# Retention norm by GpSimd and VectorE, and the second gathered chunk's x1, places and pace

## The chip, the cores and the metric

The kernel runs on one core of a Trainium2 chip. The metric is the time of one execution in microseconds on the device, as the median of the runs shown. A core has engines that run side by side, each through its own list of instructions in order: TensorE (PE in the profile; its weight loads are PEld), VectorE (DVE), ScalarE (ACT), GpSimd (POOL) and SyncE (SP), which only issues transfers. Sixteen DMA engines move the data; GpSimd issues the gathers, SyncE the rows of weights, ScalarE a few others.

## The reference, cut to what matters

One layer of a decoder for 512 prompt tokens and 32 sample tokens, D = 1024. First a mixer: four retention heads of width 128 beside a convolution of width 31, then an output projection and a layer norm, which gives x1. Then PEER, an expert retrieval: each token takes, for each of 8 heads, 16 of 16384 single-neuron experts and adds their outputs. The two places that the change touches:

```python
def head_norm(x):
    mu = jnp.mean(xf, axis=-1, keepdims=True)
    var = jnp.mean(jnp.square(xf - mu), axis=-1, keepdims=True)
    return ((xf - mu) * lax.rsqrt(var + LN_EPS)).astype(x.dtype)
...
u = jnp.take(peer_u, idx, axis=0)
act = jax.nn.gelu(jnp.einsum('phkd,pd->phk', u, xb), approximate=False)
vv = jnp.take(peer_v, idx, axis=0)
return jnp.einsum('phk,phkd->pd', gate * act, vv)
```

## The kernel before

**Tokens.** They are worked in groups: chunk 0 (128 prompt tokens), the 32 samples, chunk 1 (128), and the last 256 prompt tokens. The mixer runs for chunk 0 first, then for the other 416 tokens together. A retention chunk is `retain` (L731): `scores` (L355), `attend` (L363), `advance` (L372) and `head_norm` (L320), whose result `gate_heads` (L339) transposes on TensorE (L342) and multiplies with the gate (L343). The kernel leaves the decay of the queries out of `attend`, so its heads come out scaled by a factor per row and head; `head_norm` puts it right with the constants gq and gq2. Beside this, `silu_gate` (L243) makes the gate from a sigmoid on ScalarE (L252) and a step on VectorE (L254).

**PEER in two ways.** The first three groups fetch their experts: `gather` (L583) goes through slots k; for each, GpSimd issues an indirect transfer (L591) of 128 rows of 8 KB (u and v of one expert per token), VectorE multiplies u with x1 and sums (L597, the dot), ScalarE makes the gelu and the weight (L605, L606), VectorE adds weight times v to the accumulator (L611). Chunk 0 has 128 slots, the samples 32 (four heads' groups lie side by side in the 128 partitions), chunk 1 128. The last 256 tokens meet all experts on TensorE: `scores_of` (L815) reads a row `ut` of 512 KB and multiplies it (L822), `build` (L895) makes the selection matrices from one-hot steps on ScalarE (L902, L904) and VectorE (L906, L910) and small products (L915), and `v_products` (L936) reads a row of 512 KB and adds its products (L939) into four banks of PSUM.

**The last part.** `run` (L623, called at L1041) interleaves two generators: `phases` (L982), which issues the value rows e = 0 to 127, the second `build` and the last 32 score rows, and `fetched` (L1020), which finishes chunk 0, then gathers the samples, then chunk 1. `finish` (L614) adds x1, makes the layer norm (`layer_norm`, L446) and stores.

**Places.** A gathered slot lies in a tile of 128 x 2048 from a pool: `gp` has three; chunk 0 has one more in `gx` for its first 48 slots, chunk 1 one more in `gx2` (for k % 4 == 3). The pool `dn`, one buffer for each name, holds x1g (the x1 of the group at work, read back from `x1_dram`), and yt (the result ahead of its store).

**The pace.** `units` collects one TensorE instruction for each value row from e = 48 on (L980), each score row of the last 32 (L824) and each second of the last rows (L1017): 112 in all. For chunk 1, slot k waits for unit (k - 28)*15//14, where that is not negative (L588 to L595).

**The order.** Each engine's list is written by a scheduler that plans the whole program ahead, not by the order of the Python lines; `behind` and `hold` tie single instructions to others (the dots of chunk 0 from slot 48 on stand behind steps of the norms, `steps["p"]`). So an edit in one place can move instructions elsewhere.

## Time and profile before

| | us |
|---|---|
| median of 3 runs | 1550.36 (1547.07 to 1553.19) |
| the profiled execution | 1559.73 |
| its span, first to last instruction | 1558.0 |
| PE busy | 1479.0 (95%) |
| DVE busy | 1226.4 (79%) |
| ACT busy | 579.5 (37%) |
| POOL busy | 390.4 (25%) |
| DMA | 505.85 MB, mean 325 GB/s |

A row of the timeline gives start, duration, engine, line, operation, tiles, and in brackets how long the engine stood idle before it and what released it. A row of the chain of work that ended last gives start, duration and what it was. A busy TensorE need not be at its peak, since ends of matmuls are modelled.

### The profile page before, as it was taken

To read this page: it belongs to the slowest core of one execution; us is meant where nothing else is said; L and a number is where in the kernel's file an instruction comes from. 1 tells how busy PE (TensorE), PEld (TensorE's weight loads), DVE (VectorE), ACT (ScalarE), POOL (GpSimd) and SP (SyncE) were. 2 spreads that over 40 slices of the span, in tenths; PEclk is the share of its full clock that TensorE was granted. 3 is DMA by queue.
4 is the path that set the end of the run, shared out by engine and by line. 5 is a ranking of instruction groups with operands and counts; after the bars stand their busy time and mean duration, and the time that the engine had idled before them with its cause. 6 is when DMAs were issued, how large, how long until landed. Compare 5 with 4: busy or idle time off the path is not lost.

```text
span 1558.0 us, 20737 instructions
## 1 busy us (share of the span) xinstructions
PE 1479.0 (95%) x7046; PEld 1006.9 (65%) x7046; DVE 1226.4 (79%) x3151; ACT 579.5 (37%) x1633; POOL 390.4 (25%) x329
## 2 busy tenths in 40 slices
PE   6999989987999999899999999999999999999996
PEld 6978657555766668788878885444566666644332
DVE  3869989978756999999977989567776766766666
ACT  2224443225111333333534799424993111111111
POOL 2001225232321222312231100222223332333430
PEclk9999999998999999999999999999999999999999
DMA  9648786985689779999999723999989999999995
GB/s 351 253 152 353 253 268 235 378 346 173 238 338 346 263 264 355 346 339 350 372 358 355 278 82 130 409 336 424 356 323 403 412 424 414 411 425 411 424 419 218
DMA packets 100120, 505.85 MB, mean 325 GB/s; under 512 B 10248, under 2 KB 21256, under 8 KB 57126
## 3 DMA queue, kind: packets, MB, share of 16 engines
q0 software_dynamic: 42240, 305.12, 50.7%
q1 hardware_dynamic: 51325, 192.05, 32.4%
q10 hardware_dynamic: 6448, 7.36, 1.6%
q8 instruction: 55, 0.90, 0.2%
q14 instruction: 52, 0.42, 0.1%
HBM read 499.12 MB, written 5.80 MB: 324 GB/s over the span
## 4 chain that ended last, share of the span: by engine, by line
PE 40%; DVE 24%; DMA 18%; issue 10%; ACT 4%; POOL 3%; SPq 0%; POOLq 0%; DVEq 0%; ACTq 0%
PE sp L822 13%; PE pB L939 13%; DMA g<-in_uv_dram,Ib 7%; DVE acc L611 6%; PE mm L487 5%; DMA g<-in_uv_dram,I 5%; DVE g L597 4%; PE mm L200 4%; POOL g L591 3%; PE mm L915 2%; DMA uv<-in_ut_dram 2%; DMA g<-in_w_in_dram 2%; ACT off L902 1%; DMA uv<-in_uv_dram 1%; DVE B L910 1%
## 5 line engine op out<-in xcount | busy, mean ns | idle before, releaser
L822 PE MATMUL sp<-x1T,uv 128*128 128x256 f32 x2048 | 464.7, 383 | 5.7 <-DMA uv<-in_ut_dram 4.2
L611 DVE SCALAR_TENSOR_TENSOR acc<-g,wgt,acc 128x1024 f32<-128x1024 f32 x285 | 364.6, 1279 | 92.6 <-ACT wgt L606 91.2
L822 PEld LDWEIGHTS sp<-x1T,uv 128*128 128x128 f32 x2048 | 386.8, 192 | 76.3 <-issue 22.1
L591 POOL DMA_INDIRECT g<-in_uv_dram,I x128 | 170.7, 1333 | 461.6 <-DVE acc L611 257.9
L605 ACT ACTIVATE act<-act 128x1 f32<-128x1 f32 x288 | 57.6, 200 | 585.2 <-DVE g L597 584.9
L591 POOL DMA_INDIRECT g<-in_uv_dram,Ib x128 | 158.7, 1240 | 443.7 <-DVE acc L611 127.7
L597 DVE SCALAR_TENSOR_TENSOR g<-g,x1g 128x1024 f32<-128x1024 f32 x160 | 195.3, 1223 | 79.3 <-DMA g<-in_uv_dram,Ib 55.5
L200 PE MATMUL mm<-x1T,w 128*128 128x384 f32 (+1 forms) x512 | 178.3, 504 | 1.5 <-ACT score L536 1.3
L597 DVE SCALAR_TENSOR_TENSOR g<-g,x 128x1024 f32<-128x1024 f32 x128 | 154.8, 1215 | 28.5 <-DMA g<-in_uv_dram,I 28.4
L939 PE MATMUL pB<-uv,Ga 128*128 128x512 f32 x352 | 159.9, 599 | 1.8 <-DMA uv<-in_uv_dram 1.7
L902 ACT ACTIVATE off<-row,e1T 128x128 bf16<-128x128 bf16 x512 | 157.6, 388 | 1.0
L200 PEld LDWEIGHTS mm<-x1T,w 128*128 128x128 f32 x512 | 97.2, 192 | 73.4 <-issue 40.0
L939 PE MATMUL pB<-uv,Gd 128*128 128x512 f32 x256 | 115.2, 598 | 2.3 <-DMA uv<-in_uv_dram 1.6
L939 PEld LDWEIGHTS pB<-uv,Ga 128*128 128x128 f32 x352 | 65.0, 190 | 80.5 <-issue 64.1
L939 PE MATMUL pB<-uv,Gb 128*128 128x512 f32 x256 | 113.5, 597 | 2.4 <-DMA uv<-in_uv_dram 1.9
L939 PEld LDWEIGHTS pB<-uv,Gd 128*128 128x128 f32 x256 | 46.7, 190 | 70.6 <-issue 62.7
L939 PEld LDWEIGHTS pB<-uv,Gb 128*128 128x128 f32 x256 | 47.3, 190 | 58.0 <-issue 53.0
L915 PEld LDWEIGHTS <-A 128*128 128x128 bf16 x1536 | 60.7, 96 | 31.8 <-issue 17.6
L915 PE MATMUL mm<-B,A 128*128 128x96 bf16 (+1 forms) x1536 | 64.3, 191 | 9.3 <-DVE Gc L956 5.4
L910 DVE TENSOR_TENSOR B<-M,gtT 128x768 bf16<-128x768 bf16 (+1 forms) x192 | 69.2, 418 | 4.5 <-PE mm L915 4.5
L939 PE MATMUL pB<-uv,Gc 128*128 128x512 f32 x160 | 72.7, 600 | 0.0
L904 ACT ACTIVATE A<-off 128x1024 bf16<-128x1024 bf16 x64 | 67.4, 1054 | 10.0 <-PE mm L915 9.0
(274 smaller groups left out, 1674.7 us busy)
## 6 DMA issues: line engine op xcount, KB each, us to landing
uv<-in_uv_dram SPq DMA_DIRECT2D x132, 512.0 KB
uv<-in_ut_dram SPq DMA_DIRECT2D x128, 512.0 KB
w<-in_w_in_dram SPq DMA_DIRECT2D x18, 1024.0 KB
w<-in_w_query_dram SPq DMA_DIRECT2D x16, 1024.0 KB
w<-in_w_out_dram SPq DMA_DIRECT2D x7, 1024.0 KB
g<-in_uv_dram,I POOLq DMA_INDIRECT x128
keys<-in_state_retention_dram ACTq DMA_DIRECT2D x4, 512.0 KB
out_dram<-keys SPq DMA_DIRECT2D x4, 512.0 KB
```

Source lines behind the costliest of these rows:

```text
L200: T.matmul(p[:, :n], w[m // 2][:, k, (m % 2) * 128:(m % 2 + 1) * 128], xT[:, k, c0:c0 + n], start=(k == 0), stop=(k == 7))
L487: last = T.matmul(banks_[q][:n, s * 256:(s + 1) * 256], src[:, k, c0:c0 + n], wo[q * 2 + s][:, k0 + k, :], start=(xT is None and k0 == 4 a ...
L591: fetch = G.indirect_dma_start(out=t, out_offset=None, in_=a["uv"], in_offset=bass.IndirectOffsetOnAxis(ap=idx[:, k:k + 1], axis=0))
L597: dot = V.scalar_tensor_tensor(t[:, :D], t[:, :D], 1.0, x1, op0=OP.mult, op1=OP.mult, accum_out=act[:, 0:1])
L605: S.activation(act[:, 1:2], act[:, 0:1], AF.Gelu)
L611: V.scalar_tensor_tensor(acc, v, wgt, acc, op0=OP.mult, op1=OP.add)
L822: mm = T.matmul(sp[:, i], u[:, k], x1T[:, k, NG2:], start=(k == 0), stop=(k == 7), skip_group_check=True)
L902: S.activation(off[:, t], row, AF.Abs, bias=e1T[:, t1 + t:t1 + t + 1])
L904: S.activation(A, off, AF.Relu, bias=1.0, scale=-1.0)
L910: V.tensor_tensor(B[:, q], M, pairs_of(gtT[:, q], t1).to_broadcast([128, TB // 2, ne, 2]), op=OP.mult)
L915: mm = T.matmul(pt[:, t % nt], A[:, t - t1], B[:, q, (t - t1) // 2, :, t % 2], start=(q == 0), stop=(q == 2))
L939: ps_.append(T.matmul(pB[b][q], W[:, b * 128:(b + 1) * 128], vt[:, q * 512:(q + 1) * 512], start=False, stop=(e == NK - 1), skip_group_che ...
```

## The change

**The norm.** The factor per row and head cancels in a norm except at the small constant, so the constant is divided by its square (`ce`, made on the host) in place of multiplying the variance by gq2 and the root by gq. The root is then an addition and a power on GpSimd. Each head's result is one step on VectorE, (x - mean) * root, in place of a bias (nb) and one step on ScalarE. `steps[kind]` is now the last of these steps.

**The gathers.** Chunk 1's x1 is read into the place of chunk 0's x1 (the name `x1_0`), issued from slot 24 of the samples on, behind the end of the first build, in place of a `dn` tile after the samples are done. The pool `dn` now holds one tile of the size of a slot: first the samples' x1 in one half and the results of chunk 0 and of the samples in the other, then the fifth place of chunk 1's slots (k % 5 == 4; `gx2` is the place of k % 5 == 3). Chunk 1's result lies in a `gp` tile and is stored by ScalarE's queue. The pace is (32, 11, 10): slot k waits for unit (k - 32)*11//10, and 32 slots have none.

```diff
-PACE = (28, 15, 14)
+PACE = (32, 11, 10)
...
-    parts["gq_p"] = np.exp((i + 1.0)[:, None] * lg)
-    parts["gq2_p"] = np.exp(2 * (i + 1.0)[:, None] * lg)
+    parts["ce_p"] = EPS * np.exp(-2 * (i + 1.0)[:, None] * lg)
...
         rs = small("hrs", [128, H])
-        V.tensor_mul(rs[:n], mv[:n, :, 1], cc("gq2_" + kind)[:n])
-        rsqrt(rs[:n], rs[:n])
-        V.tensor_mul(rs[:n], rs[:n], cc("gq_" + kind)[:n])
-        nb = small("hnb", [128, H])
-        steps[kind] = V.scalar_tensor_tensor(nb[:n], mv[:n, :, 0], -1.0, rs[:n], op0=OP.mult, op1=OP.mult)
+        G.tensor_add(rs[:n], mv[:n, :, 1], cc("ce_" + kind)[:n])
+        G.tensor_tensor(rs[:n], rs[:n], mhalf[:n].to_broadcast([n, H]), op=OP.pow)
         on = small("on", [128, 512])
         for h in range(H):
-            S.activation(on[:n, h * DH:(h + 1) * DH], po[:n, h * DH:(h + 1) * DH], AF.Identity,
-                         bias=nb[:n, h:h + 1], scale=rs[:n, h:h + 1])
+            steps[kind] = V.tensor_scalar(on[:n, h * DH:(h + 1) * DH], po[:n, h * DH:(h + 1) * DH], mv[:n, h, 0:1],
+                                          rs[:n, h:h + 1], op0=OP.subtract, op1=OP.mult)
...
-            spare = gx if x1 is x1_0 and k < KX else (gx2[0] if gx2 and len(slots) == 128 else None)
-            t = (spare if spare is not None and k % 4 == 3 else gp).tile([128, 2 * D], F32, name="g")
+            if x1 is x1_0:
+                pool = gx if k < KX and k % 4 == 3 else gp
+            else:
+                pool = (gp, gp, gp, gx2[0], dn)[k % 5] if len(slots) == 128 else gp
+            t = pool.tile([128, 2 * D], F32, name="g")
...
     def fetched():
-        t = dn.tile([128, D], F32, name="yt")
+        both = dn.tile([128, 2 * D], F32, name="g")
+        x1s, t = both[:, :D], both[:, D:]
         finish(x1_0, [acc0[:, 0:512], acc0[:, 512:]], 128, [(0, 128, o[0][0, 0:128])], t)
...
+        for k, _ in enumerate(gather(x1s, Ig["s"], GTg["s"].rearrange("p h k -> p (h k)"), ac, range(NS))):
+            if k == FREE + 4:
+                x1b = per.tile([128, D], F32, name="x1_0")
+                behind(nc.scalar.dma_start(x1b, x1_dram[NS:NS + 128]), fence[0])
             yield
...
+        ac = per.tile([128, D], F32, name="acc")
+        yield from gather(x1b, Ig["b"], GTg["b"].rearrange("p h k -> p (h k)"), ac, range(128))
+        t = gp.tile([128, 2 * D], F32, name="g")[:, :D]
+        finish(x1b, [ac[:, 0:512], ac[:, 512:]], 128, [(0, 128, o[0][0, 128:256])], t, True, nc.scalar)
```

More of the change, by code (lines that the diff above doesn't have):

```diff
@@ L67, in _consts @@
     parts["kc_p"] = (DH ** -0.5) * np.exp((C - 1.0 - i)[:, None] * lg)
-    parts["gq_p"] = np.exp((i + 1.0)[:, None] * lg)
-    parts["gq2_p"] = np.exp(2 * (i + 1.0)[:, None] * lg)
+    parts["ce_p"] = EPS * np.exp(-2 * (i + 1.0)[:, None] * lg)
     for n, v in (("kc_s", (DH ** -0.5) * np.exp((SQ - 1.0 - si)[:, None] * lg)),
-                 ("gq_s", np.exp((si + 1.0)[:, None] * lg)), ("gq2_s", np.exp(2 * (si + 1.0)[:, None] * lg)),
+                 ("ce_s", EPS * np.exp(-2 * (si + 1.0)[:, None] * lg)),
                  ("blk", (sb[:, None] == np.arange(SB)[None, :]) * 1.0)):
@@ L612, in gather, with finish @@
             yield
-    def finish(x1, f, n, dsts, t, table=False):
-        for q in range(2):
-            c = slice(q * 512, (q + 1) * 512)
-            V.scalar_tensor_tensor(t[:n, c], x1[:n, c], ALPHA, f[q][:n], op0=OP.mult, op1=OP.add)
+    def finish(x1, f, n, dsts, t, table=False, q=nc.sync):
+        for h in range(2):
+            c = slice(h * 512, (h + 1) * 512)
+            V.scalar_tensor_tensor(t[:n, c], x1[:n, c], ALPHA, f[h][:n], op0=OP.mult, op1=OP.add)
         layer_norm(t, n, ln2[0], ln2[1], table=table)
         for p0, p1, dst in dsts:
-            nc.sync.dma_start(dst, t[p0:p1])
+            q.dma_start(dst, t[p0:p1])
     def run(*gens):
```

22 lines of the change are left out of this document (9 added, 13 removed).

## The prediction

> **What bounds the kernel now.** I read the span by stages first, then GpSimd's list of gathers, then the chain of work that ended last, at the two places that the change touches. The columns of the first view are the stretch, its length, the busy time of TensorE, its weight loads, VectorE, ScalarE and GpSimd, the granted clock, the DMA share and GB/s.
> ```profile
> span 1558.0 us, 20737 instructions
> ...
> 350.00:380.00 30.00, 20.16 (x103) 15.93 (x102) 26.29 (x60) 21.99 (x44) 6.57 (x8) 0.77 0.43 147
> ...
> 1100.00:1140.00 40.00, 39.73 (x317) 20.62 (x318) 30.81 (x72) 39.84 (x118) 10.00 (x7) 1.00 0.93 343
> 1140.00:1180.00 40.00, 40.00 (x359) 28.39 (x358) 27.85 (x60) 35.99 (x108) 12.01 (x10) 1.00 0.89 333
> 1180.00:1540.00 360.00, 354.09 (x1013) 187.63 (x1012) 242.14 (x308) 54.70 (x213) 112.92 (x91) 1.00 1.00 412
> 1540.00:1558.00 18.00, 7.70 (x18) 3.04 (x17) 14.75 (x25) 2.06 (x4) 0.00 (x0) 0.86 0.23 87
> ```
> Four things are to be seen. From 1180 to 1540 the DMA engines are full: 412 GB/s at a share of 1.00, so this stretch lasts as long as its bytes. From 1100 to 1180 they are not full (343 and 333 GB/s), while ScalarE, which builds the selection matrices, has no room (39.84 of 40). From 350 to 380 nothing is full: TensorE works 20.16 of 30 us and waits for the rest, which is where the heads are normalised. And in the last 18 us VectorE works 14.75.
>
> The gathers of the second chunk (slots 0 to 127) in GpSimd's list: the last without a pace (slot 27), the first with one (slot 28), and slot 127.
> ```profile
> 1129.19 1.67 POOL L591 DMA_INDIRECT g<-in_uv_dram,Ib  x1 [1.20 <-DVE acc L611]
> 1141.72 0.94 POOL L591 DMA_INDIRECT g<-in_uv_dram,Ib  x1 [10.87 <-PE pB L939]
> ...
> 1528.94 0.94 POOL L591 DMA_INDIRECT g<-in_uv_dram,Ib  x1 [2.79 <-PE pB L939]
> ```
> Slot 28 stood 10.87 us for its unit of TensorE, in the stretch where the DMA engines had room. I call 1141.72, the end of unit 0, T0. There are 112 units: 76 from rows 48 to 123 of the value products (L980), 32 score rows (L824), 4 from the last rows (L1017).
>
> **Part 1, the norm's root.** Before, the chain of a head norm is VectorE (statistics, times gq2), GpSimd (add, power), VectorE (times gq, then nb), ScalarE (four steps). After, it is VectorE (statistics), GpSimd (add, power), VectorE (four steps). The chain of work that ended last, ahead of TensorE's wait for the second norm of the three long chunks:
> ```profile
> 363.88 1.39 ACT on L335 x4
> ...
> 371.11 0.62 DVE blk L254
> 371.72 1.19 DVE acc L611
> 372.91 0.60 DVE blk L343
> 373.51 0.07 DVE hrs L330
> 373.58 1.20 DVE acc L611
> 374.78 0.09 DVE hnb L332
> 374.87 0.03 issue
> 374.89 0.47 ACT on L335
> 375.36 0.05 issue
> 375.40 0.48 PE mm L342
> ```
> The first row is the first norm's four ScalarE steps. They stand in front of the sigmoid that L254 at 371.11 waits for; they go, so L254 comes 1.39 earlier. In the order of instructions after the change, VectorE then has L254, one accumulate, the mask product of L360 and the new steps; L343 and the other accumulate stand behind them. The nearest rows for the mask product, the new step (128x128, read from PSUM), and the small steps that go:
> ```profile
> 369.17 0.68 DVE L360 TENSOR_TENSOR sc<-mm,cst 128x512 f32<-128x512 f32 x1
> ...
> L325 DVE BATCH_NORM_STATS2 hst<-mm x20: 269/282/299, 81.2 to 382.4; 128x6 f32<-128x128 f32 x16, 32x6 f32<-32x128 f32 x4
> ...
> L330 DVE TENSOR_TENSOR hrs<-hrs,cst x5: 145/155/163, 84.4 to 389.2; 128x4 f32<-128x4 f32 x4, 32x4 f32<-32x4 f32 x1
> ```
> I take 0.28 for a new step. From the sigmoid's end to TensorE it was 375.40 - 371.11 = 4.29; it becomes 0.62 + 1.19 + 0.68 + 0.28 + 0.05 = 2.82. With the 1.39 that is 1.39 + 1.47 = 2.9 us. Bounds: nothing, if the sigmoid or the scores come late for another reason, and 9.6, if both of TensorE's waits for a norm go whole:
> ```profile
> 365.32 1.12 PE L342 MATMUL mm<-cst,on 128*128 128x128 f32 x4 [2.95 <-ACT on L335]
> ...
> 375.40 0.48 PE L342 MATMUL mm<-cst,on 128*128 128x128 f32 x1 [6.65 <-ACT on L335]
> ```
> I take 3, near the sum. VectorE gains 20 steps of 0.28 and loses 15 of 0.155: 5.6 - 2.3 = 3.3 us more over five norms. I cost them at nothing: they fall where VectorE has room (26.29 of 30 in the worst stretch), and the first norm's four end before the table load and dots that ScalarE takes next. Without that cover it is 3.3. The norms of chunk 0 and of the samples I cost at nothing as well: TensorE has products of its own in front of their transposes and keeps them in that order. The new GpSimd add reads two operands where the old one read one; GpSimd finishes the root more than 3 us before it is used here, so its price doesn't count.
>
> **Part 2, the second chunk's x1, places and pace.** First the handover from the samples to the second chunk:
> ```profile
> 1026.31 5.50 DMA x1g<-x_dram
> ...
> 1035.18 1.18 POOL L591 DMA_INDIRECT g<-in_uv_dram,Ib  x1 [5.43 <-ACT act L605]
> ...
> 1063.22 0.94 POOL L591 DMA_INDIRECT g<-in_uv_dram,Ib  x1 [2.76 <-DVE acc L611]
> ```
> Today the chunk's first dots wait for its x1 (5.50 us), which waits for the samples' last reads. After, x1 lies ready, and slots 5 to 8 can be gathered some 10 us earlier; but slot 4's place holds the samples' x1 and result, so its gather waits for the samples' output. That output is ready at about 1036 (VectorE mixes four dots into the samples' norm), its transfer is below the 5.50 of a transfer four times its size, so slot 4 is issued at 1038 to 1041, against 1035.18 now. In GpSimd's order slot 4 stands behind slot 8, and slot 9, which needs slot 4's place, right behind it. By 1063 (slot 12 now) I expect the two kernels level. From there five places beat four: now slots 13 to 27 take until 1129 with four places and slot 28 stands 10.87; with five I expect slot 32 ready by T0. So four more gathers lie before T0, in the stretch at 343 GB/s: 40 us x (412 - 343) = 2.8 MB of room, 3.2 MB more at 333, for 4.2 MB. Each adds an act and a weight step on ScalarE in front of the build there:
> ```profile
> L605 ACT ACTIVATE act<-act 128x1 f32<-128x1 f32 x288 | 57.6, 200 | 585.2 <-DVE g L597 584.9
> ...
> uv<-in_uv_dram SPq DMA_DIRECT2D x132, 512.0 KB
> ```
> Two such steps are 0.4 us, times four 1.6. Part of it delays T0; I take 1 (between 0 and 1.6).
>
> Now the full stretch. A row is 512 KB, 0.524 MB; a gather is 128 rows of 8 KB, 1.049 MB. **Before**, from T0 to slot 127's issue (unit (127-28)x15//14 = 106): 106 units and 99 gathers, 55.6 + 103.8 = 159.4 MB in 1528.94 - 1141.72 = 387.2 us, 411.6 GB/s, which agrees with the windows. **After**, slot 32 is at unit 0 and slot 127 at unit (127-32)x11//10 = 104: 104 units and 95 gathers, 54.5 + 99.6 = 154.1 MB, at the same rate 374.4 us. Behind that unit stand 7 units instead of 5. The end of TensorE:
> ```profile
> 1538.88 8.82 PE L939 MATMUL pB<-uv,Gd 128*128 128x512 f32 x20 [1.63 <-DMA uv<-in_uv_dram]
> ...
> 1196.18 3.45 PE sp L822 x16
> 1199.63 3.43 PE pB L939 x8
> ```
> A unit without waits is 3.43. Before: 1538.88 + 8.82 = 1547.70, T0 + 406.0. After: 374.4 + 7 x 3.43 + the 1.63 = T0 + 400.0. That is **6.0** earlier, less 1 for T0: 5.
>
> **The tail.** The last chain on VectorE:
> ```profile
> 1548.00 0.60 DVE lst L453
> 1548.60 1.19 DVE yt L467
> 1549.79 1.32 DVE g L467 x2
> 1551.11 0.62 DVE lst L453
> ```
> Two pieces of other blocks' norms (1.19 + 1.32 = 2.5) stand between the statistics of the last block's halves, since the second chunk's last gather landed late. After, that gather is issued 7 units ahead of the end; with some 12 us to land and be added and 6 to finish it is done about 6 us before TensorE ends, and in VectorE's order the last block's statistics stand alone at the end. Gain 2.5 (0 to 2.5). The output by ScalarE's queue is off the path.
>
> **The sum.** 3 + 5 + 2.5 = 10.5 us. The profiled execution took 1559.73 (1.73 outside its span), 9.4 above the median of the runs, 1550.36; I take the difference from the median: **1539.9**. TensorE's order between 447 and 1180 moves too: two score rows (3.45 us each) go behind the start of the first build, and one row's products more stand behind the last. I cost this at nothing, between -5 and +5.
>
> **Rivals.** (a) *Full anyway.* If the four extra gathers push T0 back by their own bytes, 4.2 MB at 411.6 GB/s = 10.2 us, part 2's 6.0 turns into a loss of 4.2 and only the norm and the tail are left: 3 + 2.5 - 4.2 = 1.3 to, with half pushed back, 6.4 us, so 1544 to 1549. For it: 1040 to 1100 has little room as well. Against: slot 28's wait of 10.87 at DMA engines with room. Chance 0.22.
>
> (b) *TensorE becomes the bound.* With five requests out the engines could run fuller. From T0, 112 units x 3.43 = 384, and some 6 for ScalarE's build up to 1180: TensorE ends at T0 + 390, 16 before now, and with 3 and 2.5 the time is 1529. For it: the full stretch is 412 on average, with windows above it. Against: places don't widen engines that are full. Chance 0.10. The Trainium skill (DMA: Bandwidth & Descriptors, section "Where 436 GB/s comes from") puts the ports' ceiling at 435 GB/s and says that the HBM side binds at about 358; the trace stands above the second (412) and below the first, and at 435 the 154.1 MB would take 354 us (an estimate), less than 104 units of TensorE.
>
> (c) *Slower: the handover starves the chain.* Slot 4's gather waits for an output, slot 9 waits for slot 4 at the head of GpSimd's queue, and VectorE's order has slot 9's dot ahead of slot 7's and 8's accumulates, so for two landings of about 10 us nothing else is released. If the chain is behind the pace at T0, each slot short is a gather more in the full stretch, 1.049 / 0.4116 = 2.55 us. It decides from slot 28 at T0: four slots short are 10.2, the whole gain of 10.5. At slot 24, 8 x 2.55 = 20.4 against 10.5, the time is 1560. For it: two landings in a row without overlap. Against: slot 28 had 11 us to spare. Chance 0.12.
>
> (d) *The norm's gain is lost* and the order's moves cost up to 5: 1543 to 1548. Chance 0.09.
>
> **Numbers.** Forecast, 1533 to 1542.6: 0.45. Below 1533, by (b) or the larger norm bound: 0.12. Half a per cent, 7.8 us, is about what a measurement can tell from no change: faster, below 1542.6, is 0.57; same, to 1558.1, from (a), (d) and the mildest of (c), 0.34; slower, the rest of (c), 0.09. The range 1528 to 1554 leaves 0.1 on either side.
>
> **What would show it.** Norm: no wait of TensorE for the norm's output between 350 and 380, and the mixing products (L487) some 3 us earlier. Handover: slots 5 to 8 issued before slot 4, slot 4 at about 1038. Places: slot 32 standing for TensorE at T0. Pace: slot 127 issued some 375 us after T0, seven units before TensorE's end. Tail: no other norm between the last block's statistics. Wrong would be a released-by-VectorE slot 32 long after T0, or T0 itself late by 10.

## The result, and the profile after

| | before | changed |
|---|---|---|
| median of 6 runs, us | 1550.33 (1543.0 to 1553.19) | 1562.56 (1559.85 to 1575.23) |
| ratio to before, 95% interval | 1 | 1.0095 [1.0068, 1.0123] |
| the profiled execution, us | 1559.73 | 1564.66 |

The change makes the kernel **slower**, by 0.95% with an interval clear of 1: the medians differ by 12.2 us. The forecast was 10.5 faster, and the result lies 8.6 us above the upper end of its range.

The two profiled executions differ by only 4.9 us. That of before was 9.4 over its median, that of after 2.1 over its own: 4.9 + 9.4 - 2.1 = 12.2. So sums over the two profiles come out at 4.9, and what lies early in the span has to be compared over more profiles than two.

The same stretches of the changed kernel (columns as in the prediction):
```profile
span 1562.9 us, 20735 instructions
...
350.00:380.00 30.00, 21.35 (x107) 16.17 (x106) 28.03 (x57) 18.61 (x36) 7.02 (x7) 0.83 0.44 145
1100.00:1140.00 40.00, 37.81 (x332) 19.95 (x332) 32.01 (x68) 39.81 (x119) 13.66 (x10) 0.96 0.98 372
1140.00:1180.00 40.00, 38.56 (x323) 24.46 (x319) 30.88 (x72) 39.78 (x117) 9.79 (x8) 1.00 0.84 313
1180.00:1540.00 360.00, 358.84 (x1138) 196.31 (x1137) 240.64 (x314) 63.00 (x236) 102.83 (x91) 1.00 1.01 414
1540.00:1563.00 23.00, 15.92 (x38) 6.72 (x36) 17.33 (x28) 2.67 (x6) 0.00 (x0) 0.94 0.36 136
```
From 1100 to 1140 the DMA engines move more than before (372 for 343 GB/s), as forecast, but from 1140 to 1180 less (313 for 333), and behind 1180 they are as full as before (414 for 412). TensorE works only 37.81 and 38.56 of the two times 40 us from 1100 (before 39.73 and 40.00), and the end is later.

The gathers in GpSimd's timeline: slots 5, 4, 9, 31, 32 and 127:
```profile
1031.97 1.05 POOL L591 DMA_INDIRECT g<-in_uv_dram,Ib  x1 [8.61 <-ACT acc L609]
...
1045.93 0.94 POOL L591 DMA_INDIRECT g<-in_uv_dram,Ib  x1 [2.58 <-issue]
1063.06 1.68 POOL L591 DMA_INDIRECT g<-in_uv_dram,Ib  x1 [16.19 <-DVE acc L611]
...
1145.35 0.95 POOL L591 DMA_INDIRECT g<-in_uv_dram,Ib  x1 [3.42 <-DVE B L910]
1157.59 0.94 POOL L591 DMA_INDIRECT g<-in_uv_dram,Ib  x1 [11.29 <-PE pB L939]
...
1531.63 0.94 POOL L591 DMA_INDIRECT g<-in_uv_dram,Ib  x1 [1.95 <-PE pB L939]
```
T0, the first gather with a pace, is 1157.59 against 1141.72 before and 1139.7 in the forecast's terms. Slot 32 was ready and stood 11.29 us for its unit of TensorE: five places did bring 32 slots ahead of T0, but T0 itself is **15.9 us late**; 10 was the prediction's sign of being wrong. Behind it the forecast holds: slot 127 at T0 + 374.0 (forecast 374.4), TensorE's end at 1538.51 + 17.42 = 1555.93, T0 + 398.3 (forecast 400.0; before 406.0).

The last chain:
```profile
1538.51 17.42 PE pB L939 x40
...
1555.96 0.71 DVE lst L450
...
1556.69 0.22 DVE lmv L451
...
1556.93 1.41 DVE g L459 x2
...
1558.45 0.75 DVE g L464
1559.20 0.66 DVEq L1095
```
No other block's norm stands between the last block's statistics. TensorE's end to the end of the span is 1562.9 - 1555.93 = 7.0 for 10.3 before (1558.0 - 1547.7). So by the profiles: 15.9 for T0, less 406.0 - 398.3 = 7.7 and 3.3, is 4.9.

For the experiments I cut the way to T0 at two marks: M, the end of the mixing products (L487), and S, the issue of chunk 1's first gather (slot 3's, for the place in `gx2`), which the end of the first build releases. From M to S, before and after (two views, one of each kernel):
```profile
445.28:965.52 520.24, 499.33 (x2783) 399.97 (x2782) 465.89 (x1584) 240.19 (x643) 107.42 (x90) 0.99 0.81 302
```
```profile
440.97:970.14 529.17, 502.78 (x2784) 403.08 (x2782) 467.28 (x1584) 240.28 (x643) 103.58 (x90) 0.98 0.81 299
```
The same work takes 520.2 before and 529.2 after: 8.9 us, in a stretch to which the prediction gave nothing. TensorE is idle for 26.4 us of it in place of 20.9, and busy 3.5 us longer for the same products, at a mean granted clock of 0.98 for 0.99. From S to T0 it is 1141.72 - 965.52 = 176.2 before and 1157.59 - 970.14 = 187.5 after: 11.3 us. M itself is 4.3 earlier. These three make the 15.9.

### The profile page after: what moved, and what is told of

It reads as the page before. It is cut to its first block, busy times and chain, and to the rows that moved or that the text cites. A ratio compares the mean times of both kernels' runs of the same rounds, so it can differ in the third digit from the quotient of the medians.

```text
span 1562.9 us, 20735 instructions
## 1 busy us (share of the span) xinstructions
PE 1485.1 (95%) x7046; PEld 1016.3 (65%) x7046; DVE 1230.2 (79%) x3156; ACT 572.8 (37%) x1613; POOL 383.7 (25%) x329
## 4 chain that ended last, share of the span: by engine, by line
PE 47%; DVE 22%; DMA 14%; ACT 7%; issue 6%; POOL 2%; SPq 0%; DVEq 0%; POOLq 0%; ACTq 0%
PE pB L939 18%; PE sp L822 14%; DMA g<-in_uv_dram,I 7%; DVE acc L611 5%; PE mm L484 5%; PE mm L199 5%; DVE g L597 5%; ACT off L902 3%; DMA g<-in_uv_dram,Is 2%; DMA g<-in_uv_dram,Ib 2%; ACT A L904 2%; PE mm L915 2%; DMA g<-in_w_in_dram 2%; POOL g L591 1%; PE mm L310 1%
## 5 line engine op out<-in xcount | busy, mean ns | idle before, releaser
L822 PE MATMUL sp<-x1T,uv 128*128 128x256 f32 x2048 | 462.7, 383 | 3.9 <-ACT off L902 2.7
L822 PEld LDWEIGHTS sp<-x1T,uv 128*128 128x128 f32 x2048 | 388.4, 192 | 74.7 <-issue 12.4
L597 DVE SCALAR_TENSOR_TENSOR g<-g,x 128x1024 f32<-128x1024 f32 x256 | 311.9, 1221 | 86.8 <-DMA g<-in_uv_dram,Ib 62.7
L591 POOL DMA_INDIRECT g<-in_uv_dram,I x128 | 161.0, 1258 | 472.5 <-DVE acc L611 214.3
L591 POOL DMA_INDIRECT g<-in_uv_dram,Ib x128 | 151.5, 1183 | 458.5 <-PE pB L939 169.2
L939 PE MATMUL pB<-uv,Ga 128*128 128x512 f32 x352 | 158.4, 597 | 0.0
L939 PE MATMUL pB<-uv,Gb 128*128 128x512 f32 x256 | 113.5, 597 | 2.2 <-DMA uv<-in_uv_dram 1.8
L939 PEld LDWEIGHTS pB<-uv,Ga 128*128 128x128 f32 x352 | 65.4, 190 | 75.9 <-issue 66.5
L939 PE MATMUL pB<-uv,Gd 128*128 128x512 f32 x256 | 113.1, 596 | 0.4
L939 PEld LDWEIGHTS pB<-uv,Gd 128*128 128x128 f32 x256 | 47.2, 190 | 66.3 <-issue 58.5
L939 PEld LDWEIGHTS pB<-uv,Gb 128*128 128x128 f32 x256 | 47.2, 190 | 58.4 <-issue 52.5
L939 PE MATMUL pB<-uv,Gc 128*128 128x512 f32 x160 | 76.4, 623 | 0.0
L910 DVE TENSOR_TENSOR B<-M,gtT 128x768 bf16<-128x768 bf16 (+1 forms) x192 | 69.8, 423 | 8.1 <-PE mm L915 8.0
L904 ACT ACTIVATE A<-off 128x1024 bf16<-128x1024 bf16 x64 | 67.4, 1053 | 13.4 <-PE mm L915 12.6
L199 PE MATMUL mm<-g,w 128*128 128x160 f32 (+1 forms) x512 | 69.4, 293 | 1.3 <-DMA w<-in_w_in_dram 1.1
```

Source lines behind the costliest of these rows:

```text
L199: T.matmul(p[:, :n], w[m // 2][:, k, (m % 2) * 128:(m % 2 + 1) * 128], xT[:, k, c0:c0 + n], start=(k == 0), stop=(k == 7))
L591: fetch = G.indirect_dma_start(out=t, out_offset=None, in_=a["uv"], in_offset=bass.IndirectOffsetOnAxis(ap=idx[:, k:k + 1], axis=0))
L597: dot = V.scalar_tensor_tensor(t[:, :D], t[:, :D], 1.0, x1, op0=OP.mult, op1=OP.mult, accum_out=act[:, 0:1])
L822: mm = T.matmul(sp[:, i], u[:, k], x1T[:, k, NG2:], start=(k == 0), stop=(k == 7), skip_group_check=True)
L904: S.activation(A, off, AF.Relu, bias=1.0, scale=-1.0)
L910: V.tensor_tensor(B[:, q], M, pairs_of(gtT[:, q], t1).to_broadcast([128, TB // 2, ne, 2]), op=OP.mult)
```

## The experiments

All times are medians with a ratio to the kernel before that ran on the same chip, and its 95% interval; the other columns come from each kernel's profile. Row 52 is the first value row whose products (L939) use the second build's first tile, `Ga`; it stands a fixed number of products behind unit 0, and unlike T0 doesn't depend on slot 32.

| | ratio | us | M to S | S to row 52 |
|---|---|---|---|---|
| before, profiled twice (e5) | | 1550.33 | 520.2, 520.9 | 205.1, 206.3 |
| changed | 1.0095 [1.0068, 1.0123] | 1562.56 | 529.2 | 216.7 |
| e1 norm alone | 1.0033 [1.0012, 1.0054] | 1555.11 | 528.7 | 202.8 |
| e2 all but the norm | 1.0020 [1.0002, 1.0038] | 1553.46 | 517.4 | 217.7 |
| e3 fifth place from slot 8 | 1.0078 [1.0048, 1.0107] | 1564.02 | 529.5 | 220.6 |
| e4 one key product held | 1.0160 [1.0129, 1.0190] | 1572.68 | 535.9 | 219.4 |
| e6 norm, lists as before | 0.9974 [0.9951, 0.9997] | 1546.63 | 519.1 | 207.2 |
| e7 e3, ScalarE's acts held | 1.0104 [1.0074, 1.0134] | 1569.01 | 525.1 | 211.0 |
| e8 e7 without the norm | 1.0028 [1.0005, 1.0051] | 1553.0 | 521.4 | 210.5 |
| e9 idle copies alone | 1.0047 [1.0021, 1.0073] | 1560.17 | 528.0 | 203.7 |
| e10 x1 in place alone | 0.9984 [0.9962, 1.0006] | 1549.25 | 522.0 | 205.1 |
| e11 e2 with the old pace | 1.0063 [1.0038, 1.0089] | 1562.43 | 518.3 | 219.8 |
| e12 new pace alone | 0.9963 [0.9940, 0.9986] | 1547.0 | 523.0 | 205.3 |
| e13 e14 with e6's norm | 0.9928 [0.9904, 0.9952] | 1539.4 | 518.3 | 204.0 |
| e14 change with four places | 1.0011 [0.9984, 1.0038] | 1554.44 | 532.5 | 209.8 |
| e15 change with e6's norm | 1.0006 [0.9983, 1.0029] | 1550.3 | 517.8 | 219.6 |
| e16 e12 with e6's norm | 0.9947 [0.9921, 0.9973] | 1542.59 | 520.3 | 204.7 |
| e17 e13, fifth place from slot 32 | **0.9910 [0.9889, 0.9932]** | 1537.93 | 522.1 | 203.8 |
| e18 e13, fifth place for slots 0 to 29 | 0.9999 [0.9979, 1.0019] | 1549.9 | 522.2 | 217.7 |

The first theory had two parts. In the head, from M to S, the norm's new step makes the planner order the lists that follow in another way, and that costs; its narrow form was that one product on the sub-keys, which now comes early and stands for its keys, is the cost. At the handover, slot 4's place comes free late and the chain of gathers starves. The rivals: the steps of the norm cost by themselves; the handover's loss is the bytes of four more gathers (rival (a) of the prediction); or the pace or the new x1 is at fault.

**e1, the norm alone; e2, all but the norm.** e1 has before's `gather`, `finish`, `fetched` and pace with the changed `head_norm`; e2 is the reverse.

> The kernel before with the norm's part alone (GpSimd's root, one VectorE step per head); x1, places and pace as before. Theory H (the head loses on TensorE's order): the mixing products end about 4 us earlier, but TensorE's list then has the first products on the sub-keys 13 score instructions sooner, TensorE stands some 6 to 7 us for the keys ahead of 482, and the first build ends, with slot 3's gather of the second chunk, at 969 to 971 instead of 965.5; the time is 4 to 5 us above before's, ratio 1.003. Rival P (the prediction's part 1): 3 us below before's, ratio 0.998. Rival V (the 3.3 us of extra VectorE work count in full, no order effect): 3 us above, with the first key products no later than before.

> The change without the norm's part: before's norm, with x1 in place, five slot places and the pace from slot 32. Theory D (slot 4's dot stands first in VectorE's list, ahead of those of slots 5 to 8): slot 3's gather at 965.5 as before, slot 4 issued at about 1041, VectorE idle for 15 to 17 us around 1040 to 1055, T0 (issue of slot 32) 10 to 12 us after before's 1141.7, slot 127 374 us after T0, TensorE's end 398 us after T0; so the profile's span is within 2 us of before's 1558.0 and the time is 0 to 7 us above before's median, ratio 1.000 to 1.005. Rival F (five places pay, the prediction's part 2): 7 us below before's, ratio 0.995. Rival S (all of the loss is part 2): 12 us above, 1.008.

Each half loses by itself, e1 0.33%, e2 0.20%, and M to S is long only where the new norm is (528.7; 517.4 without). All five norms end before M, so what is lost between M and S is not the time of the norm's own steps.

**e3, the fifth place first used by slot 8.**
```diff
-                pool = (gp, gp, gp, gx2[0], dn)[k % 5] if len(slots) == 128 else gp
+                pool = ((gp, gp, gp, gx2[0])[k] if k < 4 else (gp, gp, gp, gx2[0], dn)[(k - 4) % 5]) if len(slots) == 128 else gp
```


> The change with one edit: the fifth place (that of the samples' x1 and result) is first used by slot 8 instead of slot 4. Theory D: dots 4 to 7 no longer stand behind a place that waits for the samples' output; VectorE's idle stretch of 16.8 us falls below 8, slot 9 is issued 8 to 11 us earlier than 1063, T0 comes 8 to 11 us earlier (1147 to 1150), all behind T0 as in the changed kernel, time 8 to 11 us below the changed kernel's, 1552 to 1555. Rival B (T0 is held by the second build on ScalarE and by TensorE's order, not by the gathers): T0 within 3 us of 1157.6 and the time within 3 us of 1562.6.

Slots 9 and 32 in GpSimd's timeline:
```profile
1050.49 0.94 POOL L591 DMA_INDIRECT g<-in_uv_dram,Ib  x1 [1.35 <-DVE acc L611]
...
1163.67 0.93 POOL L591 DMA_INDIRECT g<-in_uv_dram,Ib  x1 [23.83 <-PE pB L939]
```
VectorE's longest wait for a landing at the handover, first changed, then e3:
```profile
1058.06 1.23 DVE L597 SCALAR_TENSOR_TENSOR g<-g,x 128x1024 f32<-128x1024 f32 x1 [16.79 <-DMA g<-in_uv_dram,Ib]
```
```profile
1069.94 1.23 DVE L597 SCALAR_TENSOR_TENSOR g<-g,x 128x1024 f32<-128x1024 f32 x1 [8.05 <-DMA g<-in_uv_dram,Ib]
```
In the changed kernel slot 4's dot stands in VectorE's list ahead of those of slots 5 to 8, and VectorE stands 16.79 us for its landing. In e3 slot 9 comes 78.6 us after S in place of 92.9, but the trouble is halved and moved, not cured: VectorE stands 8.05 us for a later landing. T0 is no earlier: slot 32 now stands 23.83 us for TensorE. So at T0 it is not the gathers that are late but TensorE's own list; whether the handover makes that list late is taken up behind e18.

**e4, the early product on the sub-keys held back.** TensorE's waits ahead of that product, first changed, then e6, then before (timeline of each):
```profile
480.44 2.90 PE L530 MATMUL mm<-keys,qs 128*128 128x128 f32 x12 [6.69 <-DMA keys<-in_keysT_dram]
```
```profile
475.03 1.95 PE L541 MATMUL mm<-keys,qs 128*128 128x128 f32 x16
```
```profile
482.95 2.02 PE L533 MATMUL mm<-keys,qs 128*128 128x128 f32 x16 [0.58 <-DMA keys<-in_keysT_dram]
```
In the changed kernel's list 8 score instructions (L822) stand ahead of it, before 21; so it meets its keys in flight and stands 6.69 us.
```diff
+    behind(kmm[first_key], smm[23])
```


> The change with one edit: the first product on the sub-keys of the long chunks is held behind the 24th score instruction in TensorE's list (before: 21, changed: 8), nothing else. Theory H: TensorE's wait of 6.7 us ahead of 480 goes, the end of the first build (slot 3's gather) moves from 970.1 to 962 to 966, and the time is 4 to 8 us below the changed kernel's. Rival V (the VectorE steps or the gathers' landings, not TensorE's order, set the end of the first build): slot 3's gather stays within 1.5 us of 970.1 and the time within 2 us of the changed kernel's.

It got worse: 1.0160, M to S 535.9. The narrow form fell: that wait is not the cost, or what the hold moves costs more.

**e5, before again.** The unchanged kernel, profiled a second time, in one execution of 1554.14 us.

> The kernel before, unchanged, for a second profile of it. Theory J (the profiled execution of before was an untypical one): the mixing products end near 435, as in the run with the places alone, whose instructions up to there are the same, and not at 445.3; the span is 1545 to 1551 instead of 1558.0; from the end of the mixing to slot 3's gather 517 to 521, from there to T0 (slot 28) 174 to 177, from T0 to TensorE's end 402 to 407. Rival: the span is 1556 to 1560 again, and the 10 us belong to the kernel.

M at 442.41 for 445.28, M to S 520.9 for 520.2, S to T0 177.4 for 176.2: in these two profiles the stretches repeat within 1.2 us, the head up to M does not. In e2, whose lists are those of before up to M, M is at 435.01. So M in a single profile says little about the norm.

**e6, the norm with the lists as before.** GpSimd's root in all five norms; the step on VectorE in four, while the first of the three long chunks keeps nb and ScalarE's four steps. With that the lists of TensorE, VectorE, ScalarE and GpSimd from M to S are those of before, instruction by instruction.
```diff
+        if (1, 1, 0, 1, 1)[len(calls) - 1]:
+            on = small("on", [128, 512])
+            for h in range(H):
+                steps[kind] = V.tensor_scalar(on[:n, h * DH:(h + 1) * DH], po[:n, h * DH:(h + 1) * DH], mv[:n, h, 0:1],
+                                              rs[:n, h:h + 1], op0=OP.subtract, op1=OP.mult)
+            return on
```


> The norm's part in four of the five norms (GpSimd's root in all five; ScalarE's four steps with the factor and the offset stay in the first long chunk's norm alone), x1, places and pace as before. TensorE's list behind the norms is then that of before (21 score instructions ahead of the first product on the sub-keys, 488 ahead of the first build; with all five norms changed 8 and 472). Theory O (the norm's part costs by the order of the lists behind it, not by its own work): from the end of the mixing to slot 3's gather 517 to 522 as before, against 528.7 in the run with the whole norm part; time within 2 us of before's, ratio 0.998 to 1.001. Rival V (the 16 VectorE steps themselves delay what follows): 4/5 of the loss of the whole part, 525 to 528 there, ratio 1.0025 or more.

```profile
436.83:955.97 519.14, 498.39 (x2784) 399.96 (x2782) 466.58 (x1584) 240.50 (x643) 104.93 (x90) 0.99 0.81 303
```
M to S is 519.1, the kernel 0.26% faster than before (4.0 us; the prediction had 3). With all five norms, e1, it is 0.33% slower: 0.59% between two kernels that differ in one norm's four steps.

**e7 and e8, ScalarE's acts held back.** In the changed kernel and in e3 ScalarE's list has more acts ahead of the second build's steps than before's. Here the acts of slots 12 to 33 are held behind the build's steps as in before's list; e7 on e3, e8 on e3 without the norm.
```diff
+    for k, n in ((12, 38), (13, 39), (14, 40), (15, 41), (16, 43),
...
+        behind(acts[k], asteps[n])
```


> The run with the fifth place from slot 8, and one more edit: on ScalarE the activations of the second chunk's slots 12 to 33 are held behind those steps of the second build that stand ahead of the same slots before (slot 12's behind step 7 of the build, slot 13's behind step 8, and so on). Theory A (T0 is late because ScalarE, which has no room in the second build, gets to it some 10 us later, its steps standing behind activations of gathers that have not landed): ScalarE is full from 108 to 112 us after slot 3's gather (before 110, with the fifth place from slot 8 118), T0 comes 176 to 182 after slot 3's gather instead of 191.8, and the time is 5 to 10 us below that of the run with slot 8 alone, 1554 to 1559. Rival B (from slot 3's gather to the end the bytes decide, whatever T0 does): T0 earlier, but the end stays 589 to 593 after slot 3's gather and the time within 3 us of 1564.

> The change without the norm's part, the fifth place from slot 8, and the activations of slots 12 to 33 held behind the second build's steps on ScalarE as before has them. Theory A: T0 176 to 180 after slot 3's gather (189.0 with the places alone), the rest as with the places alone (T0 to TensorE's end 392 to 398), so 8 to 12 us less than with the places alone: time 1542 to 1546, ratio 0.994 to 0.997. Rival B (the bytes decide): slot 3's gather to the end stays 590 to 593, time within 2 us of 1553.5, ratio 1.001 to 1.003.

Neither wins: 1.0104 against e3's 1.0078, and 1.0028. The build gets going earlier (S + 105), and row 52 is nearly back (211.0 and 210.5), but the build takes 113 to 118 us in place of 98 to 104, and the time doesn't follow. In e7, TensorE's wait at the start of the build, and the last dot in VectorE's list ahead of the B step that it waits for (L914 is L910 of the changed kernel):
```profile
1086.95 1.15 PE L919 MATMUL mm<-B,A 128*128 128x32 bf16 x24 [9.68 <-DVE B L914]
```
```profile
1085.46 1.23 DVE L599 SCALAR_TENSOR_TENSOR g<-g,x 128x1024 f32<-128x1024 f32 x1 [3.68 <-DMA g<-in_uv_dram,Ib]
```
TensorE stands for no A of ScalarE any more, but 9.68 us (4.7 in e8) for a B of VectorE, whose step stands behind dots that wait for their landings. And slot 32 no longer goes at unit 0's end but 14.1 us later in e7, 8.0 in e8. So the wait moved from ScalarE's list to VectorE's, and ScalarE's list alone is not the cure.

**e9, idle copies in before.** Four copies of 128 x 4 per norm on VectorE, read by nobody; they turn the lists between M and S into an order near that of the changed norm, not the same (8 score instructions stand ahead of the first product on the sub-keys in both, 21 before).
```diff
+        dummy = small("hdm", [128, 4])
+        for _ in range(4):
+            V.tensor_copy(dummy[:n], mv[:n, :, 0])
```


> The kernel before with four idle VectorE copies of 128x4 added to each of the five norms, whose results nothing reads; nothing of the change. Their own work is 20 x 0.155, about 3 us of VectorE, in stages where it has room. They move the lists behind the norms to 8 score instructions ahead of the first product on the sub-keys and 472 ahead of the first build, as the whole norm part does (before 21 and 488). Theory O (the order costs): from the end of the mixing to slot 3's gather 526 to 531, time 3 to 6 us above before's, ratio 1.002 to 1.004. Rival W (work costs, not order): 519 to 523 there, time 0 to 3 us above, ratio 1.000 to 1.0015.

The copies in the groups by line, then the stretch from M to S:
```profile
L335 DVE COPY hdm<-hmv 128x4 f32<-128x4 f32 (+1 forms) x20 | 3.2, 161 | 0.1
```
```profile
445.77:973.72 527.95, 500.14 (x2783) 401.34 (x2782) 467.00 (x1584) 239.78 (x643) 105.57 (x91) 0.98 0.80 297
```
Copies of 3.2 us in all, every one done before M, make the stretch **behind** M 7 to 8 us longer (528.0; before 520.2 and 520.9) and the kernel 0.47% slower. This shows the cause in the head: it is the order of the lists. All 20 profiles agree: M to S is 517.4 to 523.0 in the 13 whose TensorE list there is before's, 525.1 to 535.9 in the 7 others. So do TensorE's waits of over 0.2 us between M and S, added up: 20.6 before, 20.6 in e6, 21.1 in e2; 26.1 changed, 25.2 in e1, 26.7 in e3, 27.4 in e9.

**e10 to e12, the places taken apart.** e10: x1 read into chunk 0's place, but four places, the old pace and the old norm. e11: e2 with the old pace. e12: before with the new pace alone.
```diff
-PACE = (28, 15, 14)
+PACE = (32, 11, 10)
```


> Of the change only the second chunk's x1 in the place of the first's (and the samples' x1 and result in one tile): four slot places as before, pace (28, 15, 14) as before, norm as before. Theory B (from slot 3's gather to the end the bytes decide): slot 9 some 5 to 10 us earlier than before against slot 3's gather, but the end 589 to 593 after it and the time within 2 us of before's. Rival F (the handover's 5 to 10 us are worth their time, the prediction's part 2): ratio 0.994 to 0.997.

> The run with the places alone (norm as before), but with before's pace (28, 15, 14): x1 in place and five slot places. Theory B: the last gather stands at unit 106 again with 5 units behind it, the stretch from slot 3's gather to the last one 563 to 566 (2.5 us, one gather's bytes, longer than with the new pace), 28 to 29 from there to the end, in sum 591 to 594, time within 2 us of the places alone's 1553.5, ratio 1.000 to 1.003. Rival T (the new pace lost what the places won, 3 us of tail): sum 586 to 589, ratio 0.997 to 0.9995.

> The kernel before with the new pace (32, 11, 10) alone. Theory B: the last gather at unit 104, 559 to 562 after slot 3's, 31 to 32 from there to the end, in sum 590 to 593, time within 2 us of before's, ratio 0.999 to 1.001; T0 (row 48's products) within 5 us of 177 after slot 3's gather, since ScalarE's list is before's. Rival T (the new pace is what delays T0 and costs): T0 185 or more, ratio 1.002 or more.

Slot 28 of e11; slot 32 of e12, and TensorE's timeline of e12 at row 48, which is unit 0:
```profile
1149.44 0.94 POOL L594 DMA_INDIRECT g<-in_uv_dram,Ib  x1 [23.32 <-PE pB L942]
```
```profile
1153.81 0.94 POOL L591 DMA_INDIRECT g<-in_uv_dram,Ib  x1 [6.76 <-PE sp L822]
```
```profile
1137.45 3.68 PE L939 MATMUL pB<-uv,Gc 128*128 128x512 f32 x8
```
e11 decides on rival (a): it has 28 slots ahead of T0 as before, so no more bytes, and T0 is 191.0 after S, later still. The five places, not the four extra gathers, are the cost: e11 against e10 is 1.0063 / 0.9984 = 1.0079, outside both of e11's expectations. In e12 the four places are not quite enough: unit 0 ends at 1137.45 + 3.68 = 1141.1 and slot 32 goes at 1153.81, 12.7 us later. (The releaser that its row names is a later unit; its own had long been done, so it stood for its place.) The kernel wins all the same, 0.37% or 5.7 us, which neither of its expectations had: the new pace **needs no fifth place**, and a chain some slots short at unit 0 didn't cost what rival (c) charges for it. x1 in place wins 0.16%, which its interval doesn't tell from nothing.

**e13 to e16, the two losers taken out.** e13: the changed kernel with four places and e6's norm. e14: with four places. e15: with e6's norm. e16: before with e6's norm and the new pace.
```diff
-                pool = (gp, gp, gp, gx2[0], dn)[k % 5] if len(slots) == 128 else gp
+                pool = (gp, gp, gp, gx2[0])[k % 4] if len(slots) == 128 else gp
```


> The change without the fifth slot place (four places, gp three times and the spare one) and with the first long chunk's norm left on ScalarE's steps: x1 in place, the new pace, GpSimd's root in all norms, VectorE's step in four of five. Theory L (two things lose, the lists' order behind the norms and the fifth place; the other edits win): the single ratios multiply, 0.9974 x 0.9984 x 0.9963 = 0.992, time 1536 to 1542; the end of the mixing to slot 3's gather 517 to 523, row 52 from 203 to 207 after slot 3's gather, the end 581 to 586 after it. Rival N (the parts take each other's place, since the full stretch absorbs what comes early): 0.996 to 0.998.

> The change with four slot places instead of five, all else as changed. Theory L: 1.0033 x 0.9984 x 0.9963 = 0.998, time 1545 to 1550; the mixing's end to slot 3's gather 527 to 531 as in the changed kernel, row 52 at 203 to 208 after slot 3's gather (changed 216.7), the end 580 to 586 after it. Rival S (the fifth place is not what delays the second build): row 52 at 213 or more, ratio 1.007 or more.

> The change with the first long chunk's norm left on ScalarE's steps, all else as changed (five places). Theory L: the head as before (the mixing's end to slot 3's gather 517 to 523 instead of 529.2), the second half as changed (row 52 at 215 to 221 after slot 3's gather, the end 591 to 594): 0.9974 x 1.002 = 0.9994, time 1547 to 1553. Rival H (the order in the head does not matter in the changed kernel, the full stretch absorbs it): time within 3 us of the changed kernel's 1562.6.

> Before with the norm's part in four of five norms and the new pace, no edit of x1 or of the places. Theory L: 0.9974 x 0.9963 = 0.9937, time 1539 to 1544. With the first run of this set it tells what x1 in place is worth: nothing (both the same), or the 0.0016 of its single run.

e13, e14, e15 and the changed kernel make a square. The fifth place costs 1.0095 / 1.0011 = 1.0084 with the new lists and 1.0006 / 0.9928 = 1.0079 with the old ones. The new lists cost 1.0095 / 1.0006 = 1.0089 with five places and 1.0011 / 0.9928 = 1.0084 with four. So, within the noise of some 0.3%, the two costs are independent and about equal, and without both the change wins 0.72%. Multiplying the single ratios gave 0.998 for e14, just below its interval, so the new lists may cost more there than between e1 and e6.

**e17 and e18, where the fifth place costs.** Both on e13: the fifth place from slot 32 on only, or for slots 0 to 29 only.
```diff
+                pool = ((gp, gp, gp, gx2[0])[k % 4] if k < 32 else (gp, gp, gp, gx2[0], dn)[(k - 32) % 5]) if len(slots) == 128 else gp
...
+                pool = ((gp, gp, gp, gx2[0], dn)[k % 5] if k < 30 else (gp, gp, gp, gx2[0])[(k - 30) % 4]) if len(slots) == 128 else gp
```


> The version with four places and one norm left on ScalarE, with the fifth place added from slot 32 on, that is behind T0 only. Theory P (the fifth place loses where it reorders the lists around the second build, not by its own transfers): the lists up to the second build's end are those with four places, row 52 starts 203 to 207 after slot 3's gather, the end 578 to 583 after it, time within 3 us of the four places' 1539.4, ratio 0.991 to 0.995. Rival Q (five requests at once slow the full stretch, whatever the lists): the end 587 to 592, ratio 0.997 to 1.001.

> The same version with the fifth place for slots 0 to 29 only, that is ahead of T0, and four places behind. Theory P: the lists around the second build are those with five places, row 52 starts 216 to 221 after slot 3's gather, the end 588 to 594 after it, ratio 0.999 to 1.002 as with five places throughout (1.0006). Rival Q: the end 578 to 584, ratio 0.992 to 0.996.

The whole cost is ahead of T0: e18 against e13 is 0.9999 / 0.9928 = 1.0072, while e17 loses nothing. 115 us from S + 100, e13, e17, e18, and changed:
```profile
1056.93:1171.93 115.00, 113.24 (x932) 65.94 (x931) 87.08 (x187) 102.86 (x299) 33.60 (x27) 1.00 0.97 375
```
```profile
1058.70:1173.70 115.00, 113.22 (x932) 65.91 (x931) 87.47 (x188) 103.47 (x301) 32.26 (x27) 1.00 0.97 384
```
```profile
1058.68:1173.68 115.00, 103.75 (x844) 58.53 (x843) 86.68 (x182) 98.66 (x290) 33.74 (x28) 0.94 0.95 359
```
```profile
1070.14:1185.14 115.00, 104.30 (x846) 59.26 (x845) 88.11 (x185) 98.51 (x290) 34.60 (x27) 0.96 0.94 361
```
With five places ahead of T0 TensorE works some 9 us less here, and the clock is below 1. e17 is the fastest kernel of the study, 0.9910; its interval overlaps e13's, so that the fifth place from slot 32 on wins anything is not shown.

How the place delays T0 can in part be followed in the changed kernel. TensorE's timeline where the second build begins:
```profile
1083.06 0.93 PE L915 MATMUL mm<-B,A 128*128 128x32 bf16 x31
1090.66 0.21 PE L915 MATMUL mm<-B,A 128*128 128x32 bf16 x1 [6.67 <-ACT A L904]
1091.23 0.95 PE L915 MATMUL mm<-B,A 128*128 128x32 bf16 x23 [0.36 <-DVE B L910]
1092.02 5.57 PE L939 MATMUL pB<-uv,Gc 128*128 128x512 f32 x8
```
TensorE stands 6.67 us for an A of ScalarE (L904). ScalarE's list there, of the changed kernel and of before:
```profile
1081.74 0.20 ACT L605 ACTIVATE act<-act 128x1 f32<-128x1 f32 x1 [2.18 <-DVE g L597]
...
1085.45 0.20 ACT L605 ACTIVATE act<-act 128x1 f32<-128x1 f32 x1 [3.19 <-DVE g L597]
...
1089.13 0.20 ACT L605 ACTIVATE act<-act 128x1 f32<-128x1 f32 x1 [3.15 <-DVE g L597]
...
1089.56 1.04 ACT L904 ACTIVATE A<-off 128x1024 bf16<-128x1024 bf16 x1
```
```profile
1072.20 0.20 ACT L605 ACTIVATE act<-act 128x1 f32<-128x1 f32 x1 [2.17 <-DVE g L597]
...
1073.91 1.06 ACT L904 ACTIVATE A<-off 128x1024 bf16<-128x1024 bf16 x1 [1.18 <-PE mm L915]
```
The A step stands in ScalarE's list behind acts of chunk 1's gathers: behind slot 13's, the fourteenth, in the changed kernel, behind slot 11's, the twelfth, before. Each act waits for a dot, each dot for a landing, and the gathers land one in 3.7 us (1081.74, 1085.45, 1089.13). But the number of acts is not the fifth place's doing. In kernels that differ in the places alone it is the same: 14 in e14 as in the changed kernel, 13 in e13 as in e15 and e18, 13 in e10 as in e11. What differs is when the acts can run. Where slot 4 has the fifth place (changed, e2, e4, e11, e15, e18), VectorE stands 16.3 to 18.4 us for slot 4's landing, as shown at e3, and chunk 1's fourteenth act comes 119 to 123 us after S. With x1 in place and four places there (e10, e13, e14, e17) no such wait of VectorE is over 3.4 us, and that act comes 110 to 112 after S.

So the build gets going (its seventh A step; the first six run ahead, within some 30 us of S) 114 to 119 us after S with five places and 106 to 112 with four, 114 in e14. From S + 60 to S + 215 TensorE stands 10.3 to 14.8 us in all with five places, e7 and e8 left out, and 0.7 to 3.5 with four. Row 52 comes 216.7 to 220.6 after S, without e7 and e8, against 202.8 to 209.8. That these waits are where TensorE stands is seen. That slot 4's late place is the whole of the cost is not shown: the lists behind the handover differ too, no run with five places ahead of T0 takes VectorE's wait away whole, and e3, which halves it, has 15 acts ahead of the A step and loses as much.

## Why the prediction was wrong

**The step on TensorE's order failed.** The prediction's words: "TensorE's order between 447 and 1180 moves too ... I cost this at nothing, between -5 and +5." It is one of the two large terms. The new order costs 0.84 to 0.89% (the square), 0.59% by e1 and e6 and 0.47% by e9, 7 to 14 us, and as much is seen between M and S (7 us from before to e9, 14 from e13 to e14). The order was read and one row's move was seen, but its price was set by the few rows that move, not by the waits that a less lucky order meets over 520 us. Which part of the lists costs stays open: e4 undid one product and lost more.

**The step on the fifth place failed.** "From there five places beat four ... with five I expect slot 32 ready by T0 ... Part of it delays T0; I take 1 (between 0 and 1.6)." The sentence ahead of it, "By 1063 (slot 12 now) I expect the two kernels level", failed first: the changed kernel issues slot 9 at 1063.06. The forecast had counted slot 4's late place, but not that VectorE's list would stand 16.79 us for it. Slot 32 was ready all the same, but T0 came 11.3 us later after S: the price counted the acts' own 0.4 us, not the landings that VectorE's dots and ScalarE's acts wait for in front of the build, slot 4's first of all. The fifth place costs 0.79 to 0.84%, 12 to 13 us; and its gain was not there to win: with four places and x1 in place (e13) slot 32 goes 178.7 after S, for 175.9 at which unit 0 ends before, and the pace wins even where it is 12.7 us late (e12).

**Rival (c) named the place and half of the mechanism.** Slot 4 was issued at 1045.93 (1038 to 1041 forecast), slot 9 at 1063.06 behind 16.19 us of idleness, and VectorE's list let nothing else through until slot 4 had landed, much as (c) had it. But its price, a gather's bytes for each slot short at T0, is not what was paid: the chain caught up and slot 32 waited for TensorE, and e12, short at unit 0, wins. The delay was passed on through the acts to the build. **Rival (a)** had the sign right; e11 rejects its bytes.

**The norm's term was right** where the order is held: 3 forecast, 0.26% or 4.0 us in e6, interval 0.5 to 7.6. The mean of M agrees: 440.2 in the six profiles with before's lists up to M, 436.5 in the six with e6's. In the change as made it is not seen: with all five norms new M is 440.7 in the mean of four (changed, e1, e3, e14). By its own steps, on the chain of the changed kernel ahead of the second long norm:
```profile
367.72 0.59 ACT sg L251
...
368.34 0.62 DVE blk L253
368.95 1.19 DVE acc L611
370.14 0.60 DVE sc L357
370.75 0.33 DVE on L332
...
371.12 0.47 PE mm L339
```
From the sigmoid's end (368.31) to TensorE it is 2.81, forecast 2.82; a new step is 0.33 for 0.28. TensorE's two waits there went from 2.95 + 6.65 = 9.6 to this:
```profile
365.14 1.89 PE L355 MATMUL mm<-blk 128*128 128x128 f32 x8 [4.55 <-DVE Rst L379]
371.12 0.47 PE L339 MATMUL mm<-cst,on 128*128 128x128 f32 x1 [4.09 <-DVE on L332]
```
4.55 + 4.09 = 8.6: the first wait is for another step of VectorE now (L379). So only about 1 of the 3 is seen here; where the rest of e6's gain lies is not told apart by these rows. The sign that the prediction named, no wait of TensorE for the norm's output, didn't come.

**The pace and the tail** were forecast at 6 + 2.5 = 8.5 behind T0. In the profiles it is 7.7 + 3.3 = 11.0 with the other parts; alone, e12, 5.7 us (interval 2.2 to 9.3).

**The sum as ratios.** From before to e13: norm -0.26% (e6), pace -0.27% (e16 / e6), x1 in place -0.19% (e13 / e16); then the new lists +0.84% (e14 / e13) and the fifth place +0.84% (changed / e14): +0.95%. The forecast of 1539.9 is near the time of e13, 1539.4, in which the terms that it counted are left and the two that it costed at 0 and 1 are gone. That it is so near is partly luck: norm, pace with the tail, and x1 are 4.0, 4.2 and 2.9 us there, for 3, 8.5 and nothing in the forecast.

## What to carry to other kernels

Where a planner writes the lists, an edit's largest cost can lie hundreds of us behind it, in another engine's order: test the order by itself, with an idle instruction that turns the lists (e9) and with the edit in all places but one (e6), before judging the edit. More buffers for a prefetch are not free even where memory is: in an in-order list the work on a buffer that comes free late holds up all that stands behind it, the work on transfers that have landed and the other engines' work behind that; give the buffers to the stretch where nothing is queued behind (e17), or none. And a term that "moves only the order" wants the length of the stretch in its range, here 1.4 to 2.7% of 520 us, not the length of the instructions moved.

## What the runs showed of the hardware

**A wait on TensorE costs more than its length.** Ten us each, around and behind the wait of 6.67:
```profile
1080.00:1090.00 10.00, 3.99 (x39) 2.06 (x37) 6.79 (x10) 1.83 (x7) 2.81 (x3) 0.95 1.02 423
1090.00:1100.00 10.00, 8.96 (x61) 4.73 (x62) 8.62 (x22) 9.97 (x29) 2.63 (x2) 0.71 1.01 418
```
The granted clock (the third value from the end) falls to 0.71 behind the wait, and eight products (L939 at 1092.02) take 5.57 for 3.68 in the next warm ones: 1.9 us on top of 6.67. The Trainium skill (TensorE: Matmul & The Clock Gate, section "What's actually happening") has the clock at half after an idle window of about 3.4 us until as long a busy one has passed; these rows agree: a mean of 0.71 over 10 us is what some 5.8 us at half give.

**The head is not repeatable.** With the same lists up to M, M lies between 435.0 (e2) and 445.3 (before) in six profiles, 10 us apart; with the same TensorE list from M to S, that stretch lies between 517.4 and 523.0 in thirteen. These executions were on different chips, so chip and execution are not told apart. A gain of 3 us in that head can't be read from two profiles, only from medians on one chip; and the 8.9 us between M and S, beyond that spread, are known from one pair of profiles to some 5 us only.
